# Forming two of the four sums of weight blocks, t3 and t4, by a transfer that adds from memory

## The chip, the cores and the metric

One Trainium2 chip; the program runs on one of its cores. The time is device microseconds of one execution; of several executions the median is given. Engines are named as the profile names them: PE (TensorE), DVE (VectorE), ACT (ScalarE), POOL (GpSimd), SP (SyncE, which here only issues transfers).

## What is computed

Two layers of a decoder trunk on 512 tokens of width 1024. Cut to what matters here:

```python
for layer in range(2):
    h = rms_norm(x, pre_norm[layer])
    proj = jnp.einsum("bsd,dp->bsp", h, w_in[layer])     # 1024 -> 8192 columns
    c_b, c_c, c_x, c_z, r_q, r_k, r_v, r_z = jnp.split(proj, cuts, axis=-1)
    y_conv = c_b * causal_depthwise_conv(c_c * c_x, conv_w[layer]) * silu(c_z)
    ret = retention_chunkwise(rotary(r_q), rotary(r_k), r_v, log_gamma)   # 8 heads of 128
    y_ret = rms_norm_per_head(ret) * silu(r_z)
    out = jnp.einsum("bse,ed->bsd", concat(y_conv, y_ret), w_out[layer])
    x = x + rms_norm(out, post_norm[layer])
```

Everything is float32; the weights are 64 MB for `w_in` and 16 MB for `w_out`.

## The kernel before, in words

**Tiles.** Every float32 product is made of three matmuls: each operand is split into a high part (`wh`, written by ACT) and the rest (`wl`, written by DVE), and `mm3` (lines 369 to 373) issues high times high (L371), low times high (L372) and high times low (L373). A weight tile is a block of 128 x 1024 numbers, 512 KB: one load by SP into a `raw` buffer (L221; nine of them, `NRAW`), one `split` (L104 on ACT, then L105 on DVE) into a `wh` and a `wl` buffer (three of each), then 12 or 24 matmuls. Such a tile is an "entry"; the list `entries` is made before anything is issued.

**Order of the work.** A layer is handled in four pairs of heads. For each pair there is a convolution product c0 (four entries), then seven products p1, p7, p6, p2, p5, p4, p3 of two entries each (u = 0, 1), then a convolution product c1. The seven products are a Strassen-like scheme for the 2 x 2 blocks of retention's projections: weight blocks are called 11, 12, 21, 22, and four products use sums of them. In the order `OTHER` these sums are formed in place, by DVE, from the `raw` buffers (line 234, `sums_to`):

- for p7: t3, block 22 := block 12 + block 22
- for p6: block 22 := block 11 - t3
- for p5: block 11 := block 11 - block 12
- for p4: t4, block 22 := block 22 + block 21

Seven of the eight pairs run in the order `OTHER`; the first pair of the second layer has its own order, `FIRST` (variable `early`), and its own formulas. With two entries to a product that is 7 x 8 + 8 = 64 additions at L234, 28 of which form t3 and t4 in the order `OTHER`.

**Look-ahead.** `step_done(i)` is called when the matmuls of entry i - 1 are issued; it calls `prepare(i + 2)`, which fetches ahead (`fetch`, up to nine entries), forms the sums up to one entry further (`sums_to`) and splits. A scheduler then sets the final order of instructions on each engine, and engines run their own lists strictly in order.

**Start of the first layer.** In the first pair p6 adds onto the PSUM result of p1, so ACT has to copy that result out first (L500, `copy("r1", ...)`), and p7 and p2 go into the PSUM banks of c0, so they need DVE to have read c0's results (`conv`, L709 to L712). `conv` multiplies by `row` and `row2`, per-token factors that come out of a chain: ACT's square sums of x (L337), `vx` (L348, DVE), `rx` (L349, a power on POOL), `rb` (L358, DVE), four transposes `psr` (L361, PE), `row` and `row2` (L364, L365, ACT).

Of the kernel before, what the change touches and what calls it, by code (L numbers as in the profile page):

```python
# [13 lines left out]
ALU = mybir.AluOpType  # L14
# [62 lines left out]
def hybrid_trunk(ctx: ExitStack, tc, x, x_t, positions, pre_g, post_g, w_in, w_out, conv_w, consts, out):  # L77
# [8 lines left out]

    nc = tc.nc
    PSUM = bass.MemoryType.PSUM  # L90

# [31 lines left out]
    loads, entries, last_use = [], [], {}  # L123

    def load(src):
        loads.append(src)
        return len(loads) - 1

    def entry(name, ls, sums, src):
        i = len(entries)  # L130
        entries.append((ls, sums, src))
        for j in list(ls) + [a for t in sums for a in t if isinstance(a, int)] + [src]:
            last_use[j] = i
        return i
# [4 lines left out]
    def order_of(l, p):  # L139
        return FIRST if l and p == 0 else OTHER  # L140

    at = {}
    for l in range(DEPTH):
        for p in range(NPAIR):
            blk = {}
            order = order_of(l, p)
            early = order.index("p6") < order.index("p7")
            for prod in order + ("c1",):
                at[l, p, prod] = len(entries)
                if prod[0] == "c":  # L150
                    for kp in range(NKP):
                        j = load(w_in[l, 4 * p + 2 + int(prod[1]), kp])
                        entry("conv", [j], [], j)
                    continue
                for u in range(2):
                    g = 4 * p
                    if prod == "p1":
                        j = load(w_in[l, g, u])
                        entry(prod, [j], [], j)
                        if not early:  # L160
                            blk[11, u] = j
                        continue
                    if prod == "p2":
                        j = load(w_in[l, g, 2 + u])
                        entry(prod, [j], [], j)
                        if not early:
                            blk[21, u] = j
                        continue
                    if prod == "p3":
                        j = load(w_in[l, g + 1, 2 + u])  # L170
                        entry(prod, [j], [], j)
                        continue
                    ls = []
                    if (12, u) not in blk:
                        if early:
                            blk[11, u] = load(w_in[l, g, u])
                            ls.append(blk[11, u])
                        blk[12, u], blk[22, u] = load(w_in[l, g + 1, u]), load(w_in[l, g + 1, 2 + u])
                        ls += [blk[12, u], blk[22, u]]
                    if early and prod == "p4":  # L180
                        blk[21, u] = load(w_in[l, g, 2 + u])
                        ls.append(blk[21, u])
                    b11, b12, b22 = blk[11, u], blk[12, u], blk[22, u]
                    if early:

                        sums = {
                            "p6": [(b11, b11, "subtract", b12), (b12, b12, "add", b22), (b22, b11, "subtract", b22)],
                            "p7": [], "p5": [], "p4": [(b22, b22, "add", blk.get((21, u)))],
                        }
                        src = {"p6": b22, "p7": b12, "p5": b11, "p4": b22}  # L190
                    else:

                        sums = {
                            "p7": [(b22, b12, "add", b22)], "p6": [(b22, b11, "subtract", b22)],
                            "p5": [(b11, b11, "subtract", b12)],
                            "p4": [(b22, b22, "add", blk[21, u])] if (21, u) in blk else None,
                        }
                        src = {"p7": b22, "p6": b22, "p5": b11, "p4": b22}
                    entry(prod, ls, sums[prod], src[prod])
        halves = (0, 1, 1) if l < DEPTH - 1 else (0, 1)  # L200
        for i, h in enumerate(halves):
            at[l, "out", i] = len(entries)
            for ep in range(NEP):
                j = load(w_out[l, h, ep])
                entry("out", [j], [], j)

    NRAW = 9
    raws, ws = {}, {}
# [12 lines left out]
                nc.sync.dma_start(out=raws[j][:, kk, :], in_=loads[j][:, kk, :])  # L221

    first_use = {}
    for i, (ls, _, _) in enumerate(entries):
        for j in ls:
            first_use[j] = i

# [2 lines left out]
    def sums_to(n):  # L230
        while summed[0] <= min(n, len(entries) - 1):
            i = summed[0]
            for dst, a, op, b in entries[i][1]:
                nc.vector.tensor_tensor(out=raws[dst], in0=raws[a], in1=raws[b], op=getattr(ALU, op))  # L234
            summed[0] += 1

    def prepare(n):
        while len(ws) <= min(n, len(entries) - 1):
            i = len(ws)
            fetch(i + 1)  # L240

            sums_to(i + 1)
            wh = wpool.tile([P, 2, 512], F32R, name=f"wh{i}", tag="wh")
            wl = wpool.tile([P, 2, 512], F32R, name=f"wl{i}", tag="wl")
            if i < NKP:
                for kk in range(2):
                    k = 2 * i + kk
                    split_scaled(hTh0[:, k, :], hTl0[:, k, :], xT[:, k, :], pre_c[:, 0, k : k + 1])
                    if i == 0:
                        split(wh[:, kk, :], wl[:, kk, :], raws[0][:, kk, :])  # L250
            if i:
                split(wh, wl, raws[entries[i][2]])
            ws[i] = (wh, wl)
            fetch(i + (3 if i < 2 else 9))
# [192 lines left out]
    def block_sums(raw, Sh, Sl):  # L447


        def blk(i, j):  # L450
            return raw[:, 4 * (j - 1) : 4 * j, 256 * (i - 1) : 256 * i]

        def parts(f, src):
            return lambda: split(Sh[:, f], Sl[:, f], src)

        def s1():
            nc.vector.tensor_tensor(out=blk(2, 2), in0=blk(2, 2), in1=blk(2, 1), op=ALU.subtract)

        def s3():
            nc.vector.tensor_tensor(out=blk(2, 1), in0=blk(2, 1), in1=blk(1, 1), op=ALU.subtract)  # L460

        def s2():
            nc.vector.scalar_tensor_tensor(
                out=blk(1, 1), in0=blk(2, 2), scalar=-1.0, in1=blk(1, 1), op0=ALU.mult, op1=ALU.subtract
            )

        def s4():
            nc.vector.tensor_tensor(out=blk(1, 2), in0=blk(1, 1), in1=blk(1, 2), op=ALU.add)

        return dict(  # L470
            s1=s1, s2=s2, s3=s3, s4=s4, p1=parts(0, blk(2, 2)), p3=parts(1, blk(2, 1)),
            p2=parts(2, blk(1, 1)), p4=parts(3, blk(1, 2)),
        )
# [323 lines left out]
    for l in range(DEPTH):  # L797
# [12 lines left out]
        for p in range(NPAIR):  # L810
            hooks, between = {}, None
            sums = block_sums(raw, Sh, Sl)
# [169 lines left out]
```

## Time and profile before

| | |
|---|---|
| median of 3 runs | 937.97 us (937.57 to 938.17) |
| the profiled execution's own time | 940.74 us |
| its span, first to last instruction | 939.0 us |
| busy: PE, DVE, ACT, POOL | 920.4, 638.2, 402.4, 26.1 us |
| read from HBM, written | 110.33 MB, 4.19 MB |

The profiled execution took 940.74 us, 2.77 us above the median of the plain runs; 939.0 us of it is the span that the rows cover. In the rows a time is counted from the span's start; `a<-b` means that a is written from b; a bracket such as `[3.10 <-ACT r L500]` is the idle time of that engine ahead of the row and the instruction that ended it. Buffer numbers are left out of the profile's names: `wh`, `wl`, `raw` and `ps` stand for many tiles. The granted clock is given as a share of 2.4 GHz, so 0.50 is 1.2 GHz.

### The profile page before, as it was taken

How to read it: one execution, taken by the hardware profiler on the slowest of the kernel's cores; microseconds unless marked ns; L12 is line 12 of the kernel's file. 1: busy time of each engine (PE TensorE's matmuls, PEld its weight loads, DVE VectorE, ACT ScalarE, POOL GpSimd, SP SyncE). 2: the span in 40 equal slices, each digit the busy share in tenths (PEclk: the TensorE clock that was granted, in tenths of full speed). 3: DMA queues.
4: the chain of work that ended last, by engine and by line, in shares of the span. 5: the costliest groups of instructions: out<-in, count | busy, mean ns of one | idle time of the engine just before them, and what ended most of it. 6: DMA issues, size and time to landing. Idle time of an engine off the chain costs nothing.

```text
span 939.0 us, 11356 instructions
## 1 busy us (share of the span) xinstructions
PE 920.4 (98%) x4434; PEld 768.0 (82%) x4434; DVE 638.2 (68%) x831; ACT 402.4 (43%) x643; POOL 26.1 (3%) x46
## 2 busy tenths in 40 slices
PE   9899999999999999999998999999999999999996
PEld 6688888888888888888887888888888888888885
DVE  6978576857684778535799784778378747893324
ACT  6653245225522564334575522552254235543221
POOL 0000000000000000000000000000000000000000
PEclk9899999999999999999998999999999999999999
DMA  9444215411531252445663731252135203425002
GB/s 348 176 155 137 68 46 179 132 48 49 198 113 45 79 191 94 147 135 166 221 207 106 224 114 46 73 196 90 45 103 189 90 23 129 163 90 185 18 1 90
DMA packets 32886, 115.27 MB, mean 123 GB/s; under 512 B 4032, under 2 KB 4160, under 8 KB 32832
## 3 DMA queue, kind: packets, MB, share of 16 engines
q1 hardware_dynamic: 32688, 114.53, 36.7%
q8 instruction: 35, 0.57, 0.3%
q14 instruction: 19, 0.16, 0.0%
q10 hardware_dynamic: 144, 0.01, 0.0%
HBM read 110.33 MB, written 4.19 MB: 122 GB/s over the span
## 4 chain that ended last, share of the span: by engine, by line
PE 93%; DVE 3%; issue 1%; ACT 1%; DMA 1%; POOL 0%; SPq 0%; DVEq 0%; POOLq 0%; ACTq 0%
PE mm L373 18%; PE mm L371 18%; PE mm L372 18%; PE ps L372 10%; PE ps L373 10%; PE ps L371 10%; PE pa L653 2%; PE pss L622 2%; PE pt L612 1%; PE pa L658 1%; DVE wl L105 1%; PE pk L635 1%; DMA raw<-in_w_in 1%; DVE raw L234 1%; PE py L689 1%
## 5 line engine op out<-in xcount | busy, mean ns | idle before, releaser
L104 ACT ACTIVATE wh<-raw 128x1024 fp32r<-128x1024 f32 (+1 forms) x221 | 232.9, 1055 | 458.0 <-PE mm L372 176.8
L105 DVE TENSOR_TENSOR wl<-raw,wh 128x1024 fp32r<-128x1024 f32 (+1 forms) x221 | 268.6, 1216 | 175.9 <-ACT wh L104 173.3
L371 PE MATMUL mm<-hTh,wh 128*128 128x512 f32 x480 | 190.3, 396 | 0.7 <-ACT wh L104 0.7
L373 PE MATMUL mm<-hTh,wl 128*128 128x512 f32 x480 | 187.6, 391 | 0.0
L372 PE MATMUL mm<-hTl,wh 128*128 128x512 f32 x480 | 187.2, 390 | 0.0
L371 PEld LDWEIGHTS mm<-hTh,wh 128*128 128x128 f32 x480 | 90.3, 188 | 19.3 <-ACT wh L104 2.0
L373 PEld LDWEIGHTS mm<-hTh,wl 128*128 128x128 f32 x480 | 90.1, 188 | 19.3 <-DVE wl L105 0.5
L372 PEld LDWEIGHTS mm<-hTl,wh 128*128 128x128 f32 x480 | 90.4, 188 | 17.7
L371 PE MATMUL ps<-wh,Sh 128*128 128x512 f32 x248 | 98.9, 400 | 5.2 <-ACT r L500 3.1
L372 PE MATMUL ps<-wl,Sh 128*128 128x512 f32 x248 | 99.0, 399 | 2.1 <-DVE wl L105 2.1
L371 PE MATMUL mm<-wh,mh 128*128 128x512 f32 x256 | 100.9, 394 | 0.0
L373 PE MATMUL mm<-wh,ml 128*128 128x512 f32 x256 | 99.8, 390 | 0.0
L372 PE MATMUL mm<-wl,mh 128*128 128x512 f32 x256 | 99.7, 389 | 0.0
L373 PE MATMUL ps<-wh,Sl 128*128 128x512 f32 x248 | 98.5, 397 | 0.0
L234 DVE TENSOR_TENSOR raw<-raw,raw 128x1024 f32<-128x1024 f32 x64 | 77.1, 1220 | 4.9 <-DMA raw<-in_w_in 4.2
L372 PE MATMUL ps<-wl,hTh 128*128 128x512 f32 x184 | 71.9, 391 | 0.0
L373 PE MATMUL ps<-wh,hTl 128*128 128x512 f32 x184 | 71.7, 390 | 0.0
L371 PE MATMUL ps<-wh,hTh 128*128 128x512 f32 x184 | 71.7, 390 | 0.0
L371 PEld LDWEIGHTS ps<-wh,Sh 128*128 128x128 f32 x248 | 47.5, 192 | 16.1 <-ACT r L500 3.5
L372 PEld LDWEIGHTS ps<-wl,Sh 128*128 128x128 f32 x248 | 47.6, 192 | 13.1 <-DVE wl L105 3.4
L373 PEld LDWEIGHTS mm<-wh,ml 128*128 128x128 f32 x256 | 48.1, 188 | 10.0
L371 PEld LDWEIGHTS mm<-wh,mh 128*128 128x128 f32 x256 | 48.1, 188 | 9.6
(169 smaller groups left out, 1060.2 us busy)
## 6 DMA issues: line engine op xcount, KB each, us to landing
raw<-in_w_in SPq DMA_DIRECT2D x151, 512.0 KB, 3.3
raw<-in_w_out SPq DMA_DIRECT2D x40, 512.0 KB, 3.3
x<-in_x SPq DMA_DIRECT2D x4, 512.0 KB, 3.7
spill<-x SPq DMA_DIRECT2D x4, 512.0 KB, 3.6
x<-spill SPq DMA_DIRECT2D x4, 512.0 KB, 3.4
out<-x SPq DMA_DIRECT2D x8, 256.0 KB, 2.0
xT<-in_x_t SPq DMA_DIRECT2D x3, 512.0 KB, 8.0
post<-in_post_norm SPq DMA_DIRECT2D x2, 512.0 KB, 3.9
```

The source lines that it names most:

```text
L104: nc.scalar.activation(out=dst_h, in_=src, func=AF.Copy)
L105: nc.vector.tensor_tensor(out=dst_l, in0=src, in1=dst_h.bitcast(F32), op=ALU.subtract)
L234: nc.vector.tensor_tensor(out=raws[dst], in0=raws[a], in1=raws[b], op=getattr(ALU, op))
L371: nc.tensor.matmul(out=ps, lhsT=ah, rhs=bh, start=first, stop=False, skip_group_check=more)
L372: nc.tensor.matmul(out=ps, lhsT=ah, rhs=bl, start=False, stop=False, skip_group_check=more)
L373: nc.tensor.matmul(out=ps, lhsT=al, rhs=bh, start=False, stop=last, skip_group_check=more)
L612: nc.tensor.transpose(out=ps[:, j, :], in_=self.O[t // 2][:, t % 2, j * P : (j + 1) * P], identity=ident)
L622: nc.tensor.matmul(out=pss[:, j, :], lhsT=self.qkT[:, 2 + h, s], rhs=self.qkT[:, h, s], start=True, stop=True)
L635: nc.tensor.matmul(out=pk[:, h, :], lhsT=self.O[t // 2][:, t % 2, s], rhs=self.V[:, t, h * HD : (h + 1) * HD], start=True, stop=True,)
L653: nc.tensor.matmul(out=pa[:, j, :], lhsT=self.sT[b][:, j, :], rhs=self.V[:, t, h * HD : (h + 1) * HD], start=True, stop=(t == 0),)
L658: nc.tensor.matmul(out=pa[:, j, :], lhsT=self.qkT[:, h, t * P : (t + 1) * P], rhs=self.S[t][:, h, :], start=False, stop=True,)
L689: nc.tensor.transpose(out=ps[:, t, :], in_=self.y[:, h, t, :], identity=ident)
```

## The change

The additions that form t3 and t4 leave DVE. In their place POOL issues, for each, a transfer from memory into the `raw` buffer with `accum_op=add`: block 22 is in the buffer, and the second block (12 for t3, 21 for t4) is read from memory once more and added while it is written. Blocks 12 and 21 are still loaded by SP as before, since p5 and p2 use them. The order `FIRST` is unchanged.

```diff
     def entry(name, ls, sums, src):
         i = len(entries)
-        entries.append((ls, sums, src))
+        entries.append((ls, sums, src, l))
...
                     if prod == "p2":
                         j = load(w_in[l, g, 2 + u])
                         entry(prod, [j], [], j)
-                        if not early:
-                            blk[21, u] = j
                         continue
...
                         sums = {
-                            "p7": [(b22, b12, "add", b22)], "p6": [(b22, b11, "subtract", b22)],
+                            "p7": [(b22, (4 * p + 1, u), "add", b22)], "p6": [(b22, b11, "subtract", b22)],
                             "p5": [(b11, b11, "subtract", b12)],
-                            "p4": [(b22, b22, "add", blk[21, u])] if (21, u) in blk else None,
+                            "p4": [(b22, (4 * p, 2 + u), "add", b22)],
                         }
...
             for dst, a, op, b in entries[i][1]:
+                if isinstance(a, tuple):
+
+                    nc.gpsimd.dma_start(out=raws[dst], in_=w_in[entries[i][3], a[0], a[1]], accum_op=ALU.add)
+                    continue
                 nc.vector.tensor_tensor(out=raws[dst], in0=raws[a], in1=raws[b], op=getattr(ALU, op))
```

In the changed file most lines stand four further down (L361 is L365 there, L105 is L107, L234 is L238, and the new transfer is L236).

The lists that the engines run are set by the scheduler, and it places more than the moved instructions anew. In all pairs but the first the lists of PE and ACT are as before, and DVE's only loses its rows. In the first pair of the first layer three places differ. SP's list is the same throughout.

**POOL, the start of the program.** `raw_148` and `raw_152` hold block 22 for u = 0 and 1, `rx` is the power on which `row` rests. Before:

```order
L349 ISA
L349 TENSOR_TENSOR rx_255<-vx_254,mhalf 128x4
L707 MEMSET u_0_369 128x2
L707 MEMSET u_1_849 128x2
L707 MEMSET u_2_1055 128x2
```

Now:

```order
L236 DMA raw_148<-in_w_in 128x1024
L236 DMA raw_152<-in_w_in 128x1024
L236 DMA raw_148<-in_w_in 128x1024
L353 ISA
L353 TENSOR_TENSOR rx_255<-vx_254,mhalf 128x4
L236 DMA raw_152<-in_w_in 128x1024
L711 MEMSET u_0_369 128x2
L711 MEMSET u_1_849 128x2
```

Three transfers now stand ahead of `rx`: both of p7 and the first of p4; the library call (`ISA`) of `rx`, too, stands behind them.

**DVE, from the first pair's factor chain to `conv`.** `wl_414` belongs to p6 (u = 1), `wl_433` to p2 (u = 0); `rb` feeds PE's transposes `psr`. Before:

```order
L350 TENSOR_TENSOR r_256<-rx_255 128x4
L352 TENSOR_TENSOR et_258<-cst,vx_254 128x32
L358 COPY rb_355<-rx_255 128x4x128
L351 TENSOR_TENSOR vt_257<-cst,r_256 128x32
L105 TENSOR_TENSOR Sl_172<-xT,Sh_171 128x1024
L105 TENSOR_TENSOR wl_414<-raw_152,wh_413 128x1024
L709 TENSOR_TENSOR cc_0_368<-mm_0_173,row_363 128x512
L711 TENSOR_TENSOR sz_0_370<-mm_1_174,row_362 128x512
L710 TENSOR_TENSOR u_0_369<-mm_0_173,cc_0_368 128x512
L712 TENSOR_TENSOR pb_0_372<-mm_1_174,row_362 128x512
```

Now:

```order
L107 TENSOR_TENSOR wl_414<-raw_152,wh_413 128x1024
L107 TENSOR_TENSOR wl_433<-raw_154,wh_432 128x1024
L354 TENSOR_TENSOR r_256<-rx_255 128x4
L362 COPY rb_355<-rx_255 128x4x128
L355 TENSOR_TENSOR vt_257<-cst,r_256 128x32
L715 TENSOR_TENSOR sz_0_370<-mm_1_174,row_362 128x512
L713 TENSOR_TENSOR cc_0_368<-mm_0_173,row_363 128x512
L716 TENSOR_TENSOR pb_0_372<-mm_1_174,row_362 128x512
L714 TENSOR_TENSOR u_0_369<-mm_0_173,cc_0_368 128x512
```

`rb` has moved behind two splits, of p6's second entry and of p2's first. On ACT `wh_432` (p2, u = 0) has likewise moved ahead of `row`; in its semaphore wait it names the last matmul of p6, whose `wh` buffer it takes over.

**PE, between p6 and p7 of the first pair.** `ps_0_0_335` is the PSUM tile of p1 and p6, `ps_0_1_400` (with `wh_328`) that of p7, `ps_0_2_478` (with `wh_432`) that of p2. Before, the transposes stand between the two entries of p6 (`wh_392`, `wh_413`):

```order
L372 MATMUL ps_0_0_335<-wl_393,Sh_171 128x512
L373 MATMUL ps_0_0_335<-wh_392,Sl_172 128x512
L361 MATMUL psr_357<-cst,rb_355 128x128 x4
L371 MATMUL ps_0_0_335<-wh_413,Sh_171 128x512
L372 MATMUL ps_0_0_335<-wl_414,Sh_171 128x512
L373 MATMUL ps_0_0_335<-wh_413,Sl_172 128x512
```

Now they stand behind p6, with three matmuls of p2 between them and p7:

```order
L376 MATMUL ps_0_0_335<-wl_414,Sh_171 128x512
L377 MATMUL ps_0_0_335<-wh_413,Sl_172 128x512
L365 MATMUL psr_357<-cst,rb_355 128x128 x4
L375 MATMUL ps_0_2_478<-wh_432,hTh_87 128x512
L376 MATMUL ps_0_2_478<-wl_433,hTh_87 128x512
L377 MATMUL ps_0_2_478<-wh_432,hTl_88 128x512
L375 MATMUL ps_0_1_400<-wh_328,Sh_171 128x512
L376 MATMUL ps_0_1_400<-wl_329,Sh_171 128x512
```

Before, ten of the twelve matmuls of p6's second entry stood between the transposes and p7; now none does. The first row of p2 waits for `pb`, the first of p7 for `u`.

## Rows read from the trace of the kernel before

**Rows 1.** The page, part 1: busy us (share of the span) and instructions of each engine.

```profile
PE 920.4 (98%) x4434; PEld 768.0 (82%) x4434; DVE 638.2 (68%) x831; ACT 402.4 (43%) x643; POOL 26.1 (3%) x46
```

**Rows 2.** Waits of PE over the span, the largest: us in total, times, longest.

```profile
PE ps L371 <- ACT r L500: 3.1, 1, 3.1
```

**Rows 3.** Timeline of PE, 34 to 54 us: start, us, instruction, idle ahead and its releaser.

```profile
37.62 0.79 PE L371 MATMUL ps<-wh,Sh 128*128 128x512 f32 x1 [3.10 <-ACT r L500]
...
43.11 1.05 PE L361 MATMUL psr<-cst,rb 128*128 128x128 f32 x4
44.45 0.50 PE L371 MATMUL ps<-wh,Sh 128*128 128x512 f32 x1 [0.29 <-ACT wh L104]
45.72 0.50 PE L372 MATMUL ps<-wl,Sh 128*128 128x512 f32 x1 [0.76 <-DVE wl L105]
...
48.13 0.39 PE L372 MATMUL ps<-wl,Sh 128*128 128x512 f32 x1
```

**Rows 4.** The page, part 5: the additions at L234 (busy us, mean ns).

```profile
L234 DVE TENSOR_TENSOR raw<-raw,raw 128x1024 f32<-128x1024 f32 x64 | 77.1, 1220 | 4.9 <-DMA raw<-in_w_in 4.2
```

**Rows 5.** The page, part 6: loads of weight blocks, median us to landing.

```profile
raw<-in_w_in SPq DMA_DIRECT2D x151, 512.0 KB, 3.3
```

**Rows 6.** DMA view, loads issued from 10 to 13.8 us: median us to landing.

```profile
raw<-in_w_in SPq DMA_DIRECT2D x3, 512.0 KB, 10.2
```

**Rows 7.** Timeline of SP: issue of block 22, u = 0 and u = 1, first pair.

```profile
10.23 0.33 SPq L221 DMA_DIRECT2D raw<-in_w_in  x1
...
12.87 0.33 SPq L221 DMA_DIRECT2D raw<-in_w_in  x1
```

**Rows 8.** Timeline of ACT, 28 to 45 us: wh of p7 (28.90, 31.85) and p6.

```profile
28.90 1.07 ACT L104 ACTIVATE wh<-raw 128x1024 fp32r<-128x1024 f32 x1 [3.42 <-PE mm L372]
...
31.85 1.05 ACT L104 ACTIVATE wh<-raw 128x1024 fp32r<-128x1024 f32 x1
...
34.56 1.06 ACT L104 ACTIVATE wh<-raw 128x1024 fp32r<-128x1024 f32 x1 [0.62 <-PE ps L373]
...
36.57 1.00 ACT L500 ACTIVATE r<-ps 128x1024 f32<-128x1024 f32 x1
...
43.34 1.06 ACT L104 ACTIVATE wh<-raw 128x1024 fp32r<-128x1024 f32 x1 [3.79 <-PE ps L373]
44.31 0.58 ACT L364 ACTIVATE row<-psr 128x512 f32<-128x512 f32 x1
```

**Rows 9.** Timeline of DVE, 41 to 47 us.

```profile
41.63 0.42 DVE L358 COPY rb<-rx 128x512 f32<-128x512 f32 x1
...
44.43 1.23 DVE L105 TENSOR_TENSOR wl<-raw,wh 128x1024 fp32r<-128x1024 f32 x1 [1.15 <-ACT wh L104]
45.58 0.68 DVE L709 TENSOR_TENSOR cc<-mm,row 128x512 f32<-128x512 f32 x1
46.18 0.68 DVE L711 TENSOR_TENSOR sz<-mm,row 128x512 f32<-128x512 f32 x1
```

**Rows 10.** Windows of PE: busy us (matmuls), PEclk granted, DMA share, GB/s.

```profile
20.00:24.00 4.00, 4.00 (x20) 1.00 1.03 410
37.60:43.10 5.50, 5.48 (x12) 0.50 0.38 118
44.40:47.00 2.60, 1.79 (x7) 1.00 0.00 0
512.60:518.00 5.40, 5.33 (x13) 0.50 0.28 97
```

**Rows 11.** Timeline of POOL: `rx` of the first layer.

```profile
39.49 1.92 POOL L349 TENSOR_TENSOR rx<-vx,mhalf 128x4 f32<-128x4 f32 x1 [39.05 <-DVE vx L348]
```

**Rows 12.** Second pair: DVE's wl of p6 (u = 0), ACT's wh of p4 (u = 0).

```profile
135.08 1.22 DVE L105 TENSOR_TENSOR wl<-raw,wh 128x1024 fp32r<-128x1024 f32 x1
...
150.52 1.06 ACT L104 ACTIVATE wh<-raw 128x1024 fp32r<-128x1024 f32 x1 [1.66 <-PE ps L373]
```

More of the change, by code (lines that the diff above doesn't have):

```diff
@@ L223, in hybrid_trunk @@
     first_use = {}
-    for i, (ls, _, _) in enumerate(entries):
+    for i, (ls, *_) in enumerate(entries):
         for j in ls:
```

## The prediction, made before the changed kernel was run

> **What bounds the kernel now.** I read the busy times first. PE is busy for 920.4 of 939.0 us, DVE for 638.2 [rows 1]: the kernel is a queue of matmuls, and an addition that leaves DVE is worth something only where PE waits for DVE. So the next view is the list of PE's waits. Its largest entry is one single wait of 3.1 us [rows 2], and it is not for DVE: it ends with ACT's copy of p1's result. The timeline of PE shows where it lies, at 37.62 us, in the first pair of the first layer [rows 3]; behind it come 0.29 us for a `wh` and 0.76 us for a `wl`, and then PE runs on. Two things follow. From about 46 us on there is next to nothing to win in the pairs that the change touches. And the first pair is the place where PE has no reserve, so a new wait there is paid in full. One more reading belongs to that place: after the idle time of 3.10 us the clock granted was 0.50, that is 1.2 GHz, for all of 37.6 to 43.1 us, and full again at 44.4; the same level shows from 512.6 to 518.0 us, at the start of the second layer [rows 10].
>
> **What leaves DVE.** 28 of the 64 additions at 1.22 us each [rows 4], 34 us of DVE's 638. None of them ends a wait of PE named above, so I cost this at nothing. Four of the 28 lie in the first pair; they don't lead to the copy for which PE waits there.
>
> **What POOL and the transfer engines get.** 28 transfers of 512 KB, 14.7 MB more on 110. In a quiet stretch such a block lands 3.3 us after its issue [rows 5]; early in the program, where the transfer engines are busy all the time at 410 GB/s [rows 10], it takes 10.2 us [rows 6]. No row shows a transfer that adds.
>
> *In the six later pairs* there is cover. p4's transfer can start when the split of p6 has read block 22, at 135.08 + 1.22 = 136.3 us in the second pair, and ACT wants the sum at 150.52 [rows 12]: 14.2 us of room for 3.3 to 10.2 us. p7's transfer has far more, since block 22 lies there long before. If the cover went, ACT's `wh` of p4 would be late, and then PE. I cost it at nothing.
>
> *In the first pair* there is little. Block 22 is issued at 10.23 us for u = 0 and at 12.87 for u = 1 [rows 7]; with 10.2 us they land at 20.4 and 23.1. If adding takes as long as a load there, the sums are ready at 30.6 and 33.3 us. ACT read them at 28.90 and 31.85 [rows 8]. So the first is 1.7 us late, ACT's list shifts by that much, and the second, wanted at 33.6 then, is just in time. ACT had 0.62 us of idle time ahead of the `wh` of p6 [rows 8]; the copy that ended at 37.57, and with it PE, moves by 1.7 - 0.6 = **1.1 us**. Ends: with 3.3 us the sums are there at 23.7 and 26.4, no delay; with twice 10.2 us the first comes at 40.8 and the second is read at 43.8, 11.3 us of delay. I take 10.2 us, from the nearest row: same size, same stretch.
>
> For the transfer alone the Trainium skill (DMA: Bandwidth & Descriptors, Anatomy of one DMA) has a fit for those that GpSimd issues, 2.0 us plus the bytes over 436 GB/s, an estimate of 3.2 us for this block. The trace agrees with that in quiet stretches alone (3.3 us); by the page the 1.1 us would fall away and the sum be 946.9.
>
> **What the new order does to PE.** This is the main term. Times below are those of the trace before, without the 1.1 us. p6's first entry ends at 43.11, where the transposes `psr` began [rows 3]. Before, `psr` (1.05 us) ran while ACT and DVE split p6's next entry, and the factor chain behind it ran while PE did ten matmuls of that entry. Now p6's second entry comes first: its first matmul at 44.45, its second at 45.72, as before, since these wait for the split and not for `psr`. From 45.72 to 48.13, the second row of p7, PE took 10 steps of 0.24 us [rows 3]; p6 now ends 11 steps after 45.72, at 48.4 us.
>
> Only then can ACT start `wh` of p2 (it takes over that buffer), and DVE's `wl` of p2 stands ahead of `rb`. From the end of p6's first entry to the end of its successor's `wl` it took 43.11 to 44.43 + 1.23 = 45.66, that is 2.55 us [rows 3, 9]. The small power product and `rb` add 0.6 us (`rb` alone 0.42 [rows 9]). So `rb` is done at 48.4 + 2.55 + 0.6 = 51.5 us, and PE stands idle from 48.4 to 51.5. `psr` takes 1.05 us at the low clock: 52.6. Then `row` starts 0.15 us behind it and takes 0.58 [rows 8], and `sz`, `cc`, `pb` follow at 0.60 us each, the last 0.68 long [rows 9]: 52.6 + 0.73 + 1.2 + 0.7 = 55.2 us. PE's next matmul waits for `pb`: a second idle time of 2.6 us. Three matmuls of p2 at the low clock, 0.43 us each, and p7 starts at 56.5. It started at 47.9; of the 8.6 us, five matmuls (1.2 us) have only moved. That leaves **7.4 us**. At the full clock `psr` and the three matmuls would take about 1.2 us less: 6.2 us is the lower end.
>
> Two idle times of some 3 us, so close together, should bring the clock down as the one of 3.10 us did. The low level lasted for 5.5 us of work and more [rows 10]. Part of that falls on idle time here; between 4 and 10 matmuls of p7 should still run at 0.43 instead of 0.24 us, 0.8 to 2 us. I take **1.5 us**.
>
> **POOL.** `rx` stands behind p4's first transfer, which waits for p6's split on DVE, and behind a library call. Before, it ran at 39.49 for 1.92 us [rows 11]. It is not needed before 48.4 + 2.55 = 51 us, so POOL has 51 - 39.5 - 1.9 = 9.6 us for issuing a transfer and for that call; SP issues one in 0.33 us [rows 7]. Cost nothing. The `u` memsets and the later powers behind transfers wait for landings that precede them by many us.
>
> On the call the Trainium skill (GPSIMD Engine Reference, Instruction dispatch) says that the first use of a freshly loaded library costs about 6 us with nothing shown for it. No run here shows it yet; by the page `rx` would end at about 47.4 instead of 41.4, the sum stays, and the reserve falls to 3.6 us, so I give a late `rx` a chance of its own.
>
> **Sum.** 1.1 + 7.4 + 1.5 = 10.0 us, from 940.74 to 950.7 for the profiled execution; that one stands 2.77 us above the median of the runs, so the median goes from 937.97 to **948.0 us**. No change means within 0.2%, 1.9 us, about what a measurement of this kernel can tell.
>
> **Rivals.**
> - *Adding is slow in the crowd.* If the engines spend double time on a transfer that reads two operands, up to 11.3 us instead of 1.1: up to 958.2. It decides from 12 us per transfer on. For: the engines are full until about 30 us [rows 10]. Against: two transfers are few among some twenty. Chance 0.16.
> - *Adding is slow everywhere.* Above 14.2 us p4's sum is late in six pairs; at 16 us up to 1.8 x 6 = 11 us more, near 959. Against: 3.3 us for a plain load [rows 5]. Chance 0.04.
> - *POOL is late.* Above 9.6 us for issue and library call, `rx` holds `rb`, one for one; with 15 us the time is 953.4. Chance 0.03.
> - *Faster: DVE's relief starts p6 earlier.* DVE runs without a pause in the first pair, and it has two additions less ahead of p6's `wl`. If that, and not ACT's copy, set p6's start, PE could lose its 3.10 + 0.29 + 0.76 us and the low clock behind it (12 matmuls at 0.46 instead of 0.24, 2.6 us): 6.8 us less, 931.2. It needs the copy to start when p1 ends, at 34.5; but ACT's `wh` of p6, released by PE, and a square sum still stand between [rows 8]. Chance 0.03.
> - *No change.* Cover that I don't see, for instance splits of p2 that run ahead of p6's end, would hide both new idle times: 937 to 939. The semaphore of `wh` for p2 names p6's last matmul, which speaks against it. Chance 0.04.
>
> **How the numbers follow.** The forecast has 0.70. It and the three slower rivals make 0.93 for slower; 0.04 no change; 0.03 faster. The forecast's own lower end is 0 + 6.2 + 0 us, 944.2; I set the range's low at 943.5. Upwards it takes in most of the first rival and the third: 957. Left out are the faster case, no change, the slowest part of the first rival and most of the second, some 0.15 together.
>
> **What would show it.** In the profile of the changed kernel: DVE's additions x36 in place of x64; a new queue with 28 transfers of 512 KB; PE idle for about 3 us ahead of `psr`, released by `rb` of DVE, and for about 2.6 us ahead of the first matmul of p2, released by `pb`; PEclk 0.50 in a second stretch after about 51 us; ACT's `wh` of p7 in the first pair waiting for the transfer by 0 to 2 us; and no idle time of PE in the later pairs. I am wrong if `psr` follows p6 without a gap, if ACT waits for p7's sums by many us, or if PE waits in p4 of later pairs.

## The result, and the profile after

The changed kernel takes 949.39 us (median of 4 runs, 948.63 to 949.79) where the kernel before takes 938.07 us on the same chip (4 runs, 937.57 to 938.32). The ratio is 1.012, with a 95% interval of 1.0103 to 1.0138: slower by 11.3 us, 9.7 to 12.9. The forecast was 948.0 us, with a range of 943.5 to 957. The profiled execution took 949.18 us, 947.3 us of it span.

In the changed kernel most lines stand four further down: L375 to L377 are the three matmuls, L106 `wh`, L107 `wl`, L238 DVE's sums, L236 the new transfer, L365 `psr`, L362 `rb`, L716 `pb`, L504 the copy `r1`. First the page of the changed kernel, part 1 (busy us, share of the span, instructions), the queues of part 3 (packets, MB, share of 16 engines), and two rows each of parts 5 and 6.

```profile
PE 921.1 (97%) x4434; PEld 767.8 (81%) x4434; DVE 607.7 (64%) x803; ACT 402.8 (43%) x643; POOL 50.5 (5%) x74
...
q1 hardware_dynamic: 32688, 114.53, 36.1%
q0 software_dynamic: 4032, 14.68, 8.8%
...
L375 PE MATMUL ps<-wh,Sh 128*128 128x512 f32 x248 | 99.4, 401 | 7.5 <-ACT r L504 4.5
L375 PE MATMUL ps<-wh,hTh 128*128 128x512 f32 x184 | 72.1, 392 | 2.7 <-DVE pb L716 2.7
...
raw<-in_w_in SPq DMA_DIRECT2D x151, 512.0 KB, 4.0
raw<-in_w_in POOLq DMA_DIRECT2D x28, 512.0 KB, 6.9
```

The change does what it says: DVE has 28 instructions and 30.5 us less than in [rows 1], POOL 28 more, and a new queue moves 28 blocks. Of the 8.3 us by which the span is longer, 7.6 are idle time of PE (947.3 - 921.1 = 26.2 us against 939.0 - 920.4 = 18.6). Where, the list of PE's waits shows (over the span: us in total, times, longest).

```profile
PE ps L375 <- ACT r L504: 4.5, 1, 4.5
PE psr L365 <- DVE rb L362: 3.5, 2, 2.8
PE ps L375 <- ACT wh L106: 2.9, 2, 1.8
PE ps L375 <- DVE pb L716: 2.7, 1, 2.7
```

The timeline of PE puts the three long ones into the first pair of the first layer (start, us, instruction, idle ahead and its releaser).

```profile
38.36 0.80 PE L375 MATMUL ps<-wh,Sh 128*128 128x512 f32 x1 [4.55 <-ACT r L504]
...
45.17 0.50 PE L375 MATMUL ps<-wh,Sh 128*128 128x512 f32 x1 [1.15 <-ACT wh L106]
46.44 0.50 PE L376 MATMUL ps<-wl,Sh 128*128 128x512 f32 x1 [0.76 <-DVE wl L107]
...
50.29 0.53 PE L377 MATMUL ps<-wh,Sl 128*128 128x512 f32 x1
53.64 0.82 PE L365 MATMUL psr<-cst,rb 128*128 128x128 f32 x4 [2.82 <-DVE rb L362]
57.15 0.77 PE L375 MATMUL ps<-wh,hTh 128*128 128x512 f32 x1 [2.70 <-DVE pb L716]
...
58.57 0.63 PE L375 MATMUL ps<-wh,Sh 128*128 128x512 f32 x1
```

Against [rows 3]: p6 starts at 38.36 and not 37.62 us; `psr` stands behind p6's second entry and waits; then PE waits again, for `pb`; and p7, which started at 47.9 us, starts at 58.57. The windows of PE over that place (us, PE, PEld, DVE, ACT, POOL busy with counts, PEclk, DMA share, GB/s):

```profile
38.40:43.80 5.40, 5.40 (x12) 3.73 (x12) 2.08 (x5) 0.94 (x2) 1.91 (x2) 0.50 0.72 166
47.20:50.80 3.60, 3.60 (x9) 2.32 (x8) 0.00 (x0) 0.00 (x0) 0.50 (x1) 0.53 0.69 113
53.60:60.80 7.20, 4.46 (x13) 3.34 (x14) 5.52 (x15) 1.71 (x3) 0.09 (x1) 0.53 0.23 74
61.00:66.00 5.00, 5.00 (x23) 4.13 (x22) 1.63 (x3) 2.96 (x6) 0.00 (x0) 1.00 0.00 1
522.70:528.10 5.40, 4.72 (x20) 3.61 (x21) 5.40 (x11) 3.41 (x4) 0.00 (x0) 1.00 0.28 97
```

The first stretch at the lower level (1.2 GHz), behind the wait for `r1`, is like the one in [rows 10]. Two more, of 0.53, follow, which the kernel before did not have there. From 61 us on nothing more is lost: in the second pair DVE's `wl` of p6 runs at 145.46 us,

```profile
145.46 1.22 DVE L107 TENSOR_TENSOR wl<-raw,wh 128x1024 fp32r<-128x1024 f32 x1
```

10.4 us after its place in [rows 12]. Near 510 us the lag is still 10.1 us (the same `wh` of ACT starts at 510.11 us before and at 520.23 us here). The spans differ by less, 947.3 - 939.0 = 8.3 us, because the execution before had a stretch of low clock at 512.6 to 518.0 us [rows 10]. The same work lies at 522.7 to 528.1 us here and has a clock of 1.00 (last window).

### The profile page after: what moved, and what is told of

The parts are those of the page before. It is cut to its first block, busy times and chain, and to the rows that moved or that the text cites. A ratio compares the mean times of both kernels' runs of the same rounds, so it can differ in the third digit from the quotient of the medians.

```text
span 947.3 us, 11439 instructions
## 1 busy us (share of the span) xinstructions
PE 921.1 (97%) x4434; PEld 767.8 (81%) x4434; DVE 607.7 (64%) x803; ACT 402.8 (43%) x643; POOL 50.5 (5%) x74
## 3 DMA queue, kind: packets, MB, share of 16 engines
q1 hardware_dynamic: 32688, 114.53, 36.1%
q0 software_dynamic: 4032, 14.68, 8.8%
## 4 chain that ended last, share of the span: by engine, by line
PE 89%; DVE 4%; issue 3%; DMA 1%; ACT 1%; POOL 0%; DVEq 0%; POOLq 0%; ACTq 0%; SPq 0%
PE mm L377 17%; PE mm L376 17%; PE mm L375 17%; PE ps L376 10%; PE ps L375 10%; PE ps L377 10%; PE pa L657 2%; PE pss L626 2%; PE pt L616 1%; DVE wl L107 1%; DMA raw<-in_w_in 1%; PE pa L662 1%; PE pk L639 1%; DVE raw L238 1%; ACT wh L106 1%
## 5 line engine op out<-in xcount | busy, mean ns | idle before, releaser
L106 ACT ACTIVATE wh<-raw 128x1024 fp32r<-128x1024 f32 (+1 forms) x221 | 233.0, 1055 | 463.9 <-PE mm L376 173.3
L107 DVE TENSOR_TENSOR wl<-raw,wh 128x1024 fp32r<-128x1024 f32 (+1 forms) x221 | 268.7, 1217 | 209.4 <-ACT wh L106 206.7
L375 PE MATMUL mm<-hTh,wh 128*128 128x512 f32 x480 | 190.2, 396 | 0.0
L377 PE MATMUL mm<-hTh,wl 128*128 128x512 f32 x480 | 187.6, 391 | 0.0
L375 PE MATMUL ps<-wh,Sh 128*128 128x512 f32 x248 | 99.4, 401 | 7.5 <-ACT r L504 4.5
L377 PEld LDWEIGHTS mm<-hTh,wl 128*128 128x128 f32 x480 | 90.1, 188 | 19.3 <-DVE wl L107 0.5
L375 PEld LDWEIGHTS mm<-hTh,wh 128*128 128x128 f32 x480 | 90.3, 188 | 18.5 <-ACT wh L106 1.2
L375 PE MATMUL mm<-wh,mh 128*128 128x512 f32 x256 | 100.9, 394 | 0.0
L377 PE MATMUL mm<-wh,ml 128*128 128x512 f32 x256 | 99.8, 390 | 0.0
L377 PE MATMUL ps<-wh,Sl 128*128 128x512 f32 x248 | 98.3, 396 | 0.0
L375 PE MATMUL ps<-wh,hTh 128*128 128x512 f32 x184 | 72.1, 392 | 2.7 <-DVE pb L716 2.7
L377 PE MATMUL ps<-wh,hTl 128*128 128x512 f32 x184 | 72.0, 391 | 0.0
L375 PEld LDWEIGHTS ps<-wh,Sh 128*128 128x128 f32 x248 | 47.7, 192 | 18.7 <-ACT r L504 5.0
L377 PEld LDWEIGHTS mm<-wh,ml 128*128 128x128 f32 x256 | 48.1, 188 | 9.9
L377 PEld LDWEIGHTS ps<-wh,Sl 128*128 128x128 f32 x248 | 47.9, 193 | 10.0
L376 PEld LDWEIGHTS mm<-wl,mh 128*128 128x128 f32 x256 | 48.1, 188 | 9.6
```

What stands on the lines that cost most here:

```text
L106: nc.scalar.activation(out=dst_h, in_=src, func=AF.Copy)
L107: nc.vector.tensor_tensor(out=dst_l, in0=src, in1=dst_h.bitcast(F32), op=ALU.subtract)
L375: nc.tensor.matmul(out=ps, lhsT=ah, rhs=bh, start=first, stop=False, skip_group_check=more)
L376: nc.tensor.matmul(out=ps, lhsT=ah, rhs=bl, start=False, stop=False, skip_group_check=more)
L377: nc.tensor.matmul(out=ps, lhsT=al, rhs=bh, start=False, stop=last, skip_group_check=more)
```

## The experiments

Three theories stand against each other. **O**: the order that the scheduler chose in the first pair makes the loss. **A**: the late sums of p7 in the crowded start make it. **T**: 28 transfers cost by themselves, in every pair. Eleven further kernels were run, and the kernel before once more. The times are medians (before_again is one run), the ratios are against the kernel before on the same chip, where its median was 938.3 to 938.7 us. The diffs are shortened.

| run | what it is | us | ratio, 95% interval |
|---|---|---|---|
| late_pairs | 24 transfers, none in the first pair | 938.08 | 0.9999 (0.999 to 1.0008) |
| first_p7 | 2 transfers: p7, first pair | 940.05 | 1.0017 (1.0008 to 1.0026) |
| dve_new_order | no transfer, new order | 948.41 | 1.0104 (1.0091 to 1.0117) |
| first_p4 | 2 transfers: p4, first pair | 948.71 | 1.0106 (1.0092 to 1.012) |
| after_rx_first | 28 transfers, another order | 942.17 | 1.0034 (1.002 to 1.0047) |
| sq_before | no transfer, squares first on ACT | 939.96 | 1.0017 (1.0008 to 1.0026) |
| sq_after | 28 transfers, the same edge | 944.16 | 1.0058 (1.0045 to 1.007) |
| x_before | no transfer, x loaded first | 936.63 | 0.9982 (0.9973 to 0.9991) |
| x_after | 28 transfers, x loaded first | 937.01 | 0.9988 (0.9979 to 0.9997) |
| xsq_before | no transfer, both | 933.48 | 0.9951 (0.9938 to 0.9964) |
| xsq_after | 28 transfers, both | 935.85 | 0.9971 (0.9959 to 0.9984) |
| before_again | the kernel before, one profile | 939.40 | one run |

### late_pairs: the transfers of the six later pairs

```diff
-"p7": [(b22, (4 * p + 1, u), "add", b22)],
+"p7": [(b22, (4 * p + 1, u) if (l or p) else b12, "add", b22)],
```

(and the same for p4.)

> The first pair of the first layer keeps its four sums on VectorE; the other six pairs form theirs by transfers (24 of the 28). PE, ACT and SP keep the order of the kernel before. Theory O (the loss is made in the first pair, by the order that the scheduler chose there): 938 us, within 1 us of before, and no new PE wait over 0.3 us after 60 us. Rival T (the 24 transfers in the steady pairs cost, since they share the DMA engines with the weight loads): 942 to 949 us, with SP loads late and PE waits on a weight split in the later pairs. Rival A (the loss comes from the late sums of p7 in the crowded start): 938 us too, so this run tells T from the other two only.

Measured 938.08 us, ratio 0.9999 (0.999 to 1.0008). T falls: 24 of the 28 transfers cost nothing that can be measured. They are not free for the queues, as the page of this run shows (part 6, median us to landing):

```profile
raw<-in_w_in SPq DMA_DIRECT2D x151, 512.0 KB, 3.9
raw<-in_w_in POOLq DMA_DIRECT2D x24, 512.0 KB, 6.7
```

A plain load takes 3.9 us there and not 3.3 [rows 5], an adding one 6.7, but PE waits for neither.

### first_p7: only the late sums of p7

```diff
-(4 * p + 1, u), "add", b22)],   # every pair
+(4 * p + 1, u) if not (l or p) else b12, "add", b22)],   # p4: VectorE everywhere
```

> Only the two sums of p7 in the first pair are transfers (2 of the 28), all else on VectorE. PE keeps the order of the kernel before; ACT moves one S split. Rival A (late p7 sums in the crowded start make the loss): 947 to 949 us. Theory O: the two transfers make the first splits of p7 late by some 0.7 and 1.5 us and p6 waits for the copy r1 1 to 1.5 us longer (3.1 to about 4.5 us); 939 us, 938.3 to 940.5. Rival T: 938 us.

Measured 940.05 us, 1.0017 (1.0008 to 1.0026), so 1.6 us (0.8 to 2.4). Its timeline of PE:

```profile
38.74 0.80 PE L377 MATMUL ps<-wh,Sh 128*128 128x512 f32 x1 [4.61 <-ACT r L506]
```

and that of ACT, with the two splits of p7:

```profile
29.85 1.06 ACT L106 ACTIVATE wh<-raw 128x1024 fp32r<-128x1024 f32 x1 [2.22 <-DMA raw<-in_w_in]
...
33.70 1.06 ACT L106 ACTIVATE wh<-raw 128x1024 fp32r<-128x1024 f32 x1 [0.81 <-DMA raw<-in_w_in]
```

Both splits wait for their transfer, and the wait for the copy `r1` behind them grew from 3.10 us [rows 3] to 4.61. The S split that moved on ACT does not explain it: it stands ahead of the first split, and ACT was idle for 2.22 us after it. A is real, and about a seventh of the loss.

### dve_new_order: the order without any transfer

An ordering edge is added to the kernel before; DVE keeps all sums.

```diff
+low = split(wh, wl, raws[entries[i][2]])
+if i == at[0, 0, "p2"]:
+    tc.add_manual_dep(rbs[0], low.name, NOSYNC, reason="order")   # rbs[0]: the copy rb
```

> No transfer at all: every sum on VectorE as before. An ordering edge alone puts the copy rb behind the low half of p2's first block; PE and ACT then have in the first pair the order of the changed kernel (psr behind p6, three matmuls of p2, then p7), and POOL and SP that of before. Theory O: 945 to 949 us (terms B and C of the prediction, 8.9 us, on 938), with a PE wait for rb of some 1 to 3 us and one for pb of some 2.7 us in the first pair and a granted clock of 0.5 for a stretch of 45 to 62 us. Rivals A and T: 938 us, since no transfer is left.

Measured 948.41 us, 1.0104 (1.0091 to 1.0117): 9.8 us with no transfer in the program. Its timeline of PE shows the two waits of the changed kernel to within 0.1 us:

```profile
36.93 0.69 PE L375 MATMUL ps<-wh,Sh 128*128 128x512 f32 x1 [3.10 <-ACT r L504]
...
50.39 0.83 PE L365 MATMUL psr<-cst,rb 128*128 128x128 f32 x4 [2.74 <-DVE rb L362]
53.92 0.77 PE L375 MATMUL ps<-wh,hTh 128*128 128x512 f32 x1 [2.70 <-DVE pb L716]
```

For most of the loss this settles it between O and the others. The profiled execution was the fastest of five, 945.95 us (the slowest took 949.74), so its rows show the two waits but not all of the 9.8 us. With first_p7 the two parts sum to 9.8 + 1.6 = 11.4 us, and the change costs 11.3; with intervals of about 1 us each, the fit is closer than could be expected.

### first_p4: which transfers bring the order

```diff
-"p4": [(b22, (4 * p, 2 + u), "add", b22)],   # every pair; p7: VectorE everywhere
+"p4": [(b22, (4 * p, 2 + u), "add", b22)] if not (l or p) else [(b22, b22, "add", blk[21, u])],
```

> Only the two sums of p4 in the first pair are transfers (2 of the 28). The scheduler gives PE and ACT the new order of the changed kernel. Theory O: the transfers themselves cost nothing, the order costs what it cost with no transfer at all (948.4 us): 947 to 949.5 us. Rivals A and T: 938 us, since p7's sums are on VectorE and the steady pairs are untouched.

Measured 948.71 us, 1.0106 (1.0092 to 1.012), the same as dve_new_order. Two transfers of 28, those of p4 in the first pair, bring the whole order with them, and beyond it they cost nothing that can be measured. Why the scheduler answers these two transfers with that order was not tried.

### after_rx_first: all transfers, another order

```diff
+with tc.issue_after(rxs[0]) if len(rxs) == 1 and a[1] > 1 else ExitStack():   # p4, first layer
     nc.gpsimd.dma_start(out=raws[dst], in_=w_in[entries[i][3], a[0], a[1]], accum_op=ALU.add)
```

> All 28 transfers of the changed kernel; only the two of p4 in the first pair are queued on POOL behind the operation rx. The scheduler then puts the copy rb and the conv ahead of p6's second block again (psr inside p6's first block, p7 ahead of the rest of p6's second). Theory O: the loss shrinks, to 940 to 945 us: term A (1 us) stays, and the four conv operations are less covered than before (2 to 5 us of PE waits for rb and pb). Rivals A and T: 948 to 950 us, since every transfer is still there.

Measured 942.17 us, 1.0034 (1.002 to 1.0047). One edge on POOL, with every transfer still there, leaves 3.2 us (1.9 to 4.4) of the 11.3. The waits of 2 to 5 us for `rb` and `pb` that were expected did not come. Between 8 and 70 us PE's list has no `rb` and no `pb`; its largest are

```profile
PE ps L377 <- ACT r L506: 4.7, 1, 4.7
PE ps L377 <- ACT wh L106: 1.3, 1, 1.3
PE ps L377 <- DVE u L716: 0.6, 1, 0.6
```

The wait for `r1` is that of first_p7 to within 0.1 us, so term A (1.6 us) is about half of what is left.

### before_again: how fixed is the low clock?

> The kernel before once more, profiled: does the low clock at 48 to 55 us and at 512 to 519 us, which the first profile of it showed, come in each execution? If the second stretch is by chance, this profile lies nearer to the median of 938.0 us than the first one's 940.7 us.

This profile took 939.40 us, span 937.5. The windows of PE (columns as above):

```profile
37.60:43.10 5.50, 3.66 (x16) 2.57 (x16) 4.59 (x10) 3.05 (x6) 2.02 (x2) 1.00 0.53 168
...
512.60:518.00 5.40, 5.40 (x16) 4.25 (x15) 4.88 (x10) 1.83 (x2) 0.00 (x0) 0.59 0.50 167
```

The 3.10 us wait for `r1` is there again, but behind it the clock is 1.00, where the first profile had 0.50 [rows 10]; PE ran ahead and met other waits (1.09 us for `rb`, 1.48 for a `wl`). (The expectation puts the first stretch at 48 to 55 us; in the first profile it lies at 37.6 to 43.1, and from 47 to 72 us the clock was 1.00.) The stretch after 512 us came again, so the expectation was wrong on it. The first stretch does not come in each execution, and the profile of the changed kernel shows that the second need not come either. In the second pair this execution is 1.7 us ahead of the first profile:

```profile
133.41 1.22 DVE L105 TENSOR_TENSOR wl<-raw,wh 128x1024 fp32r<-128x1024 f32 x1
```

against 135.08 us in [rows 12]. It is likely, but not shown, that the median of 938 us belongs to executions with little of the low clock: the plain runs have no profile.

### sq_before and sq_after: the squares first

ACT's four square sums head the chain to `rx`, `row` and the conv. An edge queues the following splits behind them, in either kernel.

```diff
+if len(pin) == NT:                        # pin: the four square sums of the first layer
+    with tc.issue_after(pin[-1]):
+        nc.scalar.activation(out=dst_h, in_=src, func=AF.Copy)
```

> No transfer; in the kernel before, the weight and S splits traced after the four square sums are queued on ACT behind them, so that ACT does the squares at about 20 to 25 us and not at 31 to 38 us. rx, rb and the conv of the first tile then come early, and the scheduler keeps the program's order of products: p1 with psr inside, p7, p6, p2. Theory O (what this stretch costs is set by the order, and the first pair of the kernel before is not at its best either): the 3.1 us wait for the copy r1 and the 0.8 us for the low half go, about 2 us of waiting for the conv come in; 934 us, 932 to 937. Rivals A and T say nothing on it: 938 us if the order does not matter.

> The same edge in the changed kernel, with all 28 transfers. PE and ACT have in the first pair the order of the run without transfers beside it, so the two differ by the transfers alone. Theory O: the difference of 11.3 us shrinks to 0.5 to 4 us: the second split of p7 waits for its transfer (33.3 us in the changed kernel), and row and the conv stand behind it on ACT and DVE; 935 to 940 us, so no slower than the kernel before by more than 2 us. Rivals A and T: the transfers cost the same 11 us in any order; 943 to 949 us.

Measured 939.96 us and 944.16 us. Both expectations were wrong. sq_before is slower by 1.6 us, not faster by 4. sq_after lies outside the 935 to 940 us of O and inside the 943 to 949 that A and T gave, and the two differ by 4.2 us where O had 0.5 to 4. The timeline of ACT shows what none of the three theories had, first without transfers:

```profile
27.26 1.06 ACT L343 ACTIVATE jx<-x_-1_0_207 128x1024 bf16<-128x1024 f32 x1 [7.14 <-DMA x_-1_0_207<-in_x]
28.60 1.06 ACT L343 ACTIVATE jx<-x_-1_1_209 128x1024 bf16<-128x1024 f32 x1 [0.19 <-DMA x_-1_1_209<-in_x]
```

and with them:

```profile
29.43 1.06 ACT L347 ACTIVATE jx<-x_-1_0_207 128x1024 bf16<-128x1024 f32 x1 [9.50 <-DMA x_-1_0_207<-in_x]
...
33.33 1.06 ACT L347 ACTIVATE jx<-x_-1_1_209 128x1024 bf16<-128x1024 f32 x1 [2.75 <-DMA x_-1_1_209<-in_x]
```

The x tiles stand behind the first weight blocks in SP's list and are not there before 27 us. Two adding transfers in the full stretch make the second tile 4.7 us later, and the two runs differ by 4.2 us. PE's waits for `rb` show the same, 2.7 and 7.7 us. So the crowd can cost more than A, where something urgent stands behind the transfers. In the changed kernel as it was, x came late too (its first tile was issued at 16.39 us and took 14.9), but ACT came to it at 31.45 us and did not wait. T gains nothing by this: late_pairs above and x_after below have the transfers at no cost that can be measured.

### x_before, x_after: x loaded first

```diff
-fetch(i + (3 if i < 2 else 9))
+fetch(i + (3 if i < 3 else 9))
...
-                    0: [load_rest],
+                load_rest()               # ahead of the first run_units
```

> No transfer. The kernel before with SP's loads in another order: the four x tiles and the constants go ahead of the four blocks that p7 needs, not behind them (in the run with the squares first, ACT stood 7.1 us for the first x tile). x then lands by about 22 us and not 27 to 31, the squares end by about 26 us, and the scheduler takes the program's order p1 with psr inside, p7, p6, p2. Theory O: psr waits for nothing, p7 waits some 2 to 3 us for the conv and its own sums, the waits of 3.1 us for the copy r1, 1.9 us for low halves and 1.1 us for rb go; 935 us, 933.5 to 937.5. Against it: if what bounds this stretch is the bytes that must land before p7, not their order, 938 us or more.

> The same order of loads with all 28 transfers. PE has the order of the run without transfers beside it, and rx stands ahead of all four transfers of the first pair, so neither the order nor the x tiles are touched by them. Left is that the sums of p7 come later, as each transfer starts only when the plain load of its other block has landed and takes 7 to 10 us there: p7 starts 1 to 4 us later than in the run beside it; 936 to 940 us, against 949.4 us of the changed kernel. Theory T (the 28 transfers cost by themselves): 944 us or more.

Measured 936.63 us (0.9982, 0.9973 to 0.9991) and 937.01 us (0.9988, 0.9979 to 0.9997). With the program's order of products and x out of the way, 28 transfers make a difference of 0.4 us, less than the intervals can tell, where the change as it was costs 11.3. The longest wait of PE in the first pair is another one in each. Without transfers:

```profile
38.29 0.47 PE L371 MATMUL ps<-wh,Sh 128*128 128x512 f32 x1 [3.88 <-DVE u L710]
```

With them:

```profile
37.19 0.50 PE L375 MATMUL ps<-wh,Sh 128*128 128x512 f32 x1 [2.65 <-ACT wh L106]
```

In the first, p7's two sums stand in DVE's list ahead of and between the conv's operations, and PE waits for DVE; in the second DVE has let them go, `u` is early, and PE waits for the split of the late sum. Here, and in the pair of runs below, the relief of DVE is worth something, and the late transfer takes it back. x_after's expectation met the time but not the way: p7 starts 1.1 us earlier than in the run beside it, not 1 to 4 us later, and what it gains is lost behind it, for instance 0.76 us for a `wl`. The 0.4 us are thus a balance of a gain and a loss.

### xsq_before, xsq_after: both

> No transfer; x loads first as beside it, and the squares also queued ahead of the splits on ACT as in the run with the squares first. Theory O: little different from x loads first alone, within 1.5 us, since ACT is idle where x lands: 934 to 937 us. If slower than it, the splits queued behind the squares are what is late.

> All 28 transfers with x loaded first and the squares ahead of the splits on ACT: the fastest order of the runs so far, with the changed kernel's sums. PE has the order of the run without transfers (933.5 us). Theory O: only the late sums of p7 are left, a PE wait of 2 to 3.5 us for the split of p7 at about 34 us where the run beside it waits 2.2 us for the conv; 933.5 to 936.5 us, faster than the kernel before. Theory T: 943 us or more.

Measured 933.48 us (0.9951, 0.9938 to 0.9964) and 935.85 us (0.9971, 0.9959 to 0.9984), both faster than both kernels of the change. xsq_before is the fastest, 4.6 us under before, and outside its own expectation (934 to 937) on the good side; it was to lie within 1.5 us of x_before and is 3.2 us faster. Its window 38 to 46 us shows what it has beyond x_before; first xsq_before, then x_before:

```profile
38.00:46.00 8.00, 8.00 (x37) 6.61 (x36) 8.00 (x8) 4.70 (x5) 0.00 (x0) 1.00 0.00 0
```

```profile
38.00:46.00 8.00, 7.71 (x27) 6.29 (x28) 7.55 (x8) 2.46 (x3) 0.00 (x0) 0.79 0.07 19
```

Ahead of that window PE waited 2.20 us for `u`, not 3.88, and the clock stays at 1.00, so ten matmuls more fit into the same 8 us. The start of p7, first in xsq_before, then in xsq_after:

```profile
36.91 0.47 PE L378 MATMUL ps<-wh,Sh 128*128 128x512 f32 x1 [2.20 <-DVE u L717]
```

```profile
36.95 0.49 PE L382 MATMUL ps<-wh,Sh 128*128 128x512 f32 x1 [2.06 <-ACT wh L110]
38.21 0.50 PE L383 MATMUL ps<-wl,Sh 128*128 128x512 f32 x1 [0.76 <-DVE wl L113]
```

With the transfers p7 starts at the same time and then waits for the low half of the late sum. By the ratios xsq_after is 1.9 us slower than xsq_before, just clear of the two intervals. So in the best order found the 28 transfers do cost a little.

## Why the prediction was right

**What bounds it.** Right. The later pairs had nothing to win and nothing to lose (late_pairs 0.9999), and the first pair paid in full.

**What leaves DVE: nothing.** Right for this kernel: 30.5 us less on DVE, and no wait of PE shorter for it. The faster rival, that p6 would start earlier, did not come; the copy still stood behind ACT's list.

**Term A, p7's sums in the crowd: 1.1 us.** Right in mechanism, a little small: 1.6 us (0.8 to 2.4) by first_p7. In the changed kernel the two transfers took 9.9 us, for which 10.2 had been taken, and ACT read the sums at 29.54 and 33.31 us; forecast were 30.6 and 33.3. In detail the forecast had the first sum late and the second just in time; ACT waited for both, 2.24 and 0.73 us. The rival "adding is slow in the crowd" fell with this. Adding is slower than a plain load over the whole program (6.9 us against 4.0), but far below the 14.2 us from which the second rival counts. The estimate from the Trainium skill (DMA: Bandwidth & Descriptors, Anatomy of one DMA), 3.2 us for such a block and the 1.1 us gone, does not hold here: these two took 9.9 us, and 6.9 us is the median of all 28. The 3.3 us beside which the forecast put it are plain loads issued by SP.

**Term B, the new order: 7.4 us, and term C, the low clock: 1.5 us.** Together 8.9, measured 9.8 (8.5 to 11.0) by dve_new_order. The idle time ahead of `psr` was 2.82 us (forecast 3.1), that for `pb` 2.70 (2.6). What term C did not have: the clock fell already at 47 us, in p6's second entry, so p6 ended near 50.8 and not, with its later start of 0.7, at 49.1. That is 1.7 us. Of p7 only six matmuls ran at up to 0.43 in place of 0.24 us, 1.1 us; so the low clock cost some 2.8 us beside the waits and not 1.5. The early fall is not in each execution: in dve_new_order and first_p4 the clock was 0.99 and 0.97 from 47.0 to 50.8 us and 0.50 from there to 53.6, as the forecast had it. The sum of the forecast was 10.0 us, the trace has 10.4 in the second pair: 0.7 for the later start of p6, 2.8 for the clock, and so some 6.9 for the order, where the forecast had 1.1, 1.5 and 7.4. The mechanism was the forecast's; that the sum came closer than its parts was luck.

**POOL: nothing.** Right. `rx` ran at 40.34 for 1.04 us, directly behind a transfer's issue of 0.86 us, and its first reader on DVE came at 53.09. The 6 us for a loaded library that the Trainium skill (GPSIMD Engine Reference, Instruction dispatch) gives do not show in this trace.

**The base.** The forecast put the sum on an execution of 940.74 us and carried its 2.77 us of surplus down to the median. The 10.4 us, too, are counted from that execution. before_again is 1.7 us ahead of it in the second pair: 0.7 us by the end of p1, the rest where its clock stayed at 1.00 behind the wait for `r1`. Counted from before_again the changed kernel is 12.1 us late in the second pair and 9.8 us at the end (949.18 against 939.40), since both executions of before have the low clock after 512 us. The changed kernel was within 0.3 us of its median when profiled. That a sum of 10.0 us came within 1.3 us of the medians' 11.3 is thus in part the luck of the execution that was profiled.

## What to carry to other kernels

A scheduler that places instructions anew can turn a small change into another program: compare the lists of instructions first, and cost the moved rows before the ones that the diff names. A change that frees an engine is worth something only where that engine ends a wait, and a reordering can be tried alone, with an edge and none of the change. Where the transfer engines are full, look for what stands behind the new transfers in the queues.

## What the runs showed of the hardware that was not expected

- A transfer that adds, issued by POOL, takes 1.7 times as long as a plain one issued by SP: 6.9 us against 4.0 us for 512 KB in the same run. It takes 1.9 times the engines' time per MB: 8.8% for 14.68 MB against 36.1% for 114.53 MB, 0.60% per MB against 0.32%. No run has plain transfers of POOL, so what is due to the adding and what to POOL's queue is not told apart. The plain loads beside them are slower: their median is 3.3 us in each kernel with none or two adding transfers, 3.9 to 4.2 us in each with 24 or 28. POOL spends 0.86 to 1.05 us on the issue, SP 0.33.
- The same wait does not always bring the clock down. Behind 3.10 us of idle time at the same place the granted clock was 0.50 in the profiles of before and first_p4, low for a part of the stretch in dve_new_order (0.74 from 37.6 to 43.1 us), and 1.00 in before_again and late_pairs. In the second layer waits of 1.76 and 0.95 us stand ahead of the stretch of 0.50 in before, and waits of 1.77 and 0.95 us ahead of the same work in the changed kernel, where the clock was 1.00. Waits of 2.1 to 2.2 us at 34 to 37 us left it at 1.00 (xsq_before, xsq_after); behind one of 2.11 us at 41.7 us in sq_before it was 0.60 from 42 to 46 us. What decides was not tried, and stays open.
